# A second-level product for pairs of values units, rope pairs in another order, and a table of priority shifts

## The chip, the cores and the metric

The kernel runs on one core of a Trainium2 chip. The metric is the time of one execution in microseconds, as the device reports it; below 0.2% two versions of this kernel can't be told apart. Five engines work beside each other, each through its own instructions in order: PE (TensorE, matmuls), DVE (VectorE), ACT (ScalarE), POOL (GpSimd) and SP (SyncE, which issues the transfers here).

## The reference, cut to what matters

Two requests of 512 tokens go through the same trunk of two layers, a differential attention and a two-way retention. Each begins with one wide projection of the normalised input, and this projection is what the change is about:

```python
def trunk(x, ...):
    h = rms_norm(x, norm_g[0], NORM_EPS)
    x = x + diff_attention(h, da_w_in[0], ..., da_w_out[0], lambda_init)
    h = rms_norm(x, norm_g[1], NORM_EPS)
    x = x + bidir_retention(h, ret_w_in[0], ..., ret_w_out[0])
    return rms_norm(x, final_norm_g, NORM_EPS)

# in either mixer
proj = h @ w_in                      # 512 x 1024 by 1024 x 8192 (layer 1) or 6144 (layer 2)
q, k, v, gate = jnp.split(proj, ...) # q, k are rotated; v is used as it is; silu(gate) scales the output
```

All is float32. The two requests share the weights, so the projection is one product with 1024 tokens.

## The kernel before

**Products.** A float32 value is split into an upper part and a rest (`hi_of` on ACT, `lo_of` on DVE), and a product is three matmul passes (`PASSES`: upper by upper, upper by rest, rest by upper). On top of that the projection uses Strassen's scheme in Winograd's form: tokens, the 1024 rows of the weights and a unit's columns are halved, and a unit needs seven products P1 to P7 of half size instead of eight (`SEQ`). The token side is prepared once per layer by `make_b`, in blocks B11, B21, T1, T2, B22, T3, T4 (`B_OF`). The weights' side (sums and differences of quarters, then the split) is prepared by `Unit.prep` for each product.

**Units.** A unit is a strip of weight columns with one purpose. *Rope* units hold q or k, which are rotated (`rot_done`); *gate* units hold the gate (`gate_done`); both are of kind "pair", and their products are 12 matmuls of 128x512. *Wide* units hold values (`v_done`): they take the tokens as the stationary side, are twice as broad, and a product is 48 matmuls of 128x256 in two banks.

**Second level.** Two rope units next to each other share P2 (the product with B21): a `Duo` sees their two strips of weights as one matrix, applies Winograd's scheme once more, and does two P2 (24 matmuls of 128x512) as seven inner products of 6 matmuls of 128x256. Its operands are prepared in parts D0 to D3 (`Duo.part`) from the strips' quarters a11 to a22; the token side is cut by `inner_blocks` into t1 to t4. Wide units and single gates do P2 in full.

**Order of the units.** `mixed` puts five gates first, then the ropes in twos, with a wide unit or a gate between, and two gates last. With R, g and w for a rope, gate and wide unit the layers read

```
layer 1: g g g g g  RR w  RR g  RR RR w  RR w  RR RR w  RR  g g
layer 2: g g g g g  RR w g  RR w  RR w  RR w  g g
```

`product_order` lays out the products: a unit's last one, P4, stands behind the first of the next unit ("tail"). `projections` prepares weights ahead of PE as long as the tiles of the prepared products fit into `PROJ_WS` buffers (ws); the raw weights land in four buffers of 512 KB before that (`raw_t`).

**What sets the order on the engines.** Nothing runs at once: each operation goes to a `Plan` with its cost and what it reads and writes. `Plan.arrange` then lays the operations out by a list scheduler: PE keeps its order but for a window, the other engines take the ready operation that is due first, where the due time is counted back from the PE products that need it. `Plan.issue` repeats this eight times, keeps the shortest layout and writes the instructions out in that order, engine by engine. The order on each engine is fixed then.

**Banks.** Results stand in eight banks: three "pj", two "sc", two "o", one "tp". P1, P6, P7 and P4 of a unit add up in a pj bank (two for a wide unit), P5 and P3 in sc, P2 in o. A bank is free again when ACT and DVE have read it. P4 is handed over in its bank: `v_done` reads it twice, by `hi_of` (L439) and `lo_of` (L442).

**Lines of the profile.** L712 is a product of a rope or gate unit, L722 one of a wide unit, L874 an inner product of a Duo, L1318 the transposes of x for `make_b`, L502 its blocks. L773 adds a product to a kept one. L442 is `lo_of`, L439 `hi_of`, L425 and L423 are scalings on DVE and ACT, L1194 is the power that turns a row's sum of squares into its scale, on POOL. L1155 is the output projection, L1160 adds its result to x.

## Time and profile before

| what | value |
|---|---|
| median of 3 runs | 1796.06 us (1795.7 to 1797.08) |
| the profiled execution | 1796.09 us, its span 1794.1 us |
| busy: PE, PEld, DVE, ACT, POOL | 99%, 88%, 85%, 51%, 7% |
| instructions: PE, DVE, ACT, POOL | 10533, 2635, 1952, 256 |
| HBM | 209.55 MB read, 117.44 MB written |

The stages are, by PE's timeline: start and first projection to 640 us, attention with its output projection to 1021, second projection to some 1470, retention and the end. How to read: a row of a timeline gives start, length and engine, the line of the kernel, what is written from what, the tile's shape and the count, and in brackets how long the engine was idle before and who ended that. Matmuls are pipelined, so their price is the distance between starts.

### The profile page before, as it was taken

The page shows a single profiled execution, that of the slowest core. Times are in us where ns is not written, and L with a number is a line of the kernel's source. Part 1 is how long each engine was busy: PE and PEld are TensorE (multiplying, and loading weights), DVE is VectorE, ACT ScalarE, POOL GpSimd, SP SyncE. Part 2 cuts the span into 40 slices and gives each one's busy share as a digit, 9 for nine tenths or more (in the row PEclk, how much of TensorE's full clock was granted, in tenths as well). Part 3 has the DMA queues.
Part 4 walks back from the last instruction along what each step waited for, and adds up shares of the span by engine and source line. Part 5 has one row for each costly group of instructions (what it writes and reads, how often), then busy time and mean ns, then how long its engine had stood idle before and what let it go on. Part 6 is the DMA issues. An engine that isn't in the chain of part 4 may idle for free.

```text
span 1794.1 us, 28748 instructions
## 1 busy us (share of the span) xinstructions
PE 1778.4 (99%) x10533; PEld 1569.9 (88%) x10533; DVE 1532.6 (85%) x2635; ACT 917.8 (51%) x1952; POOL 120.6 (7%) x256
## 2 busy tenths in 40 slices
PE   9999999999999999999999999999999999999998
PEld 7789888989899888888888878898989988888887
DVE  8978899887897888888888798887988977888887
ACT  8664454444444555555455776444444455444446
POOL 1000000000000011111111200000000000111114
PEclk9999999999999999999999999999999999999999
DMA  6336454546364695555453524473746569664652
GB/s 219 120 114 196 153 170 141 181 149 202 112 181 164 196 350 184 186 188 188 168 187 127 188 65 159 130 236 105 235 139 225 165 216 404 238 234 176 229 217 94
DMA packets 162821, 328.86 MB, mean 183 GB/s; under 512 B 12773, under 2 KB 76921, under 8 KB 162681
## 3 DMA queue, kind: packets, MB, share of 16 engines
q1 hardware_dynamic: 162352, 326.71, 53.7%
q8 instruction: 82, 1.34, 0.3%
q14 instruction: 59, 0.48, 0.1%
q10 hardware_dynamic: 328, 0.34, 0.1%
HBM read 209.55 MB, written 117.44 MB: 182 GB/s over the span
## 4 chain that ended last, share of the span: by engine, by line
PE 89%; DVE 6%; DMA 2%; issue 1%; ACT 1%; SPq 1%; POOL 0%; DVEq 0%; POOLq 0%; ACTq 0%
PE pj L712 20%; PE pj L1155 19%; PE sc L712 11%; PE pj L722 6%; PE o L712 5%; PE o L1483 5%; PE sc L1422 5%; PE o L874 3%; PE sc L722 3%; PE o L1692 2%; PE o L722 2%; DVE ws L442 1%; PE sc L1648 1%; PE tp L1672 1%; PE o L1700 1%
## 5 line engine op out<-in xcount | busy, mean ns | idle before, releaser
L1155 PE MATMUL pj<-ws,arena 128*128 128x512 f32 x1542 | 377.9, 392 | 0.0
L1155 PEld LDWEIGHTS pj<-ws,arena 128*128 128x128 f32 x1542 | 281.8, 188 | 54.6 <-DVE m L989 0.3
L712 PE MATMUL pj<-b,ws 128*128 128x512 f32 x1080 | 263.1, 391 | 0.0
L712 PEld LDWEIGHTS pj<-b,ws 128*128 128x128 f32 x1080 | 199.5, 188 | 39.8
L439 ACT CAST ws<-st 128x512 fp32r<-128x512 f32 (+1 forms) x260 | 153.4, 601 | 145.9 <-PE o L874 42.1
L1160 DVE SCALAR_TENSOR_TENSOR b<-pj,pad,b 128x512 f32<-128x512 f32 (+1 forms) x257 | 191.1, 746 | 26.0 <-PE pj L1155 23.6
L442 DVE TENSOR_TENSOR ws<-st,ws 128x512 fp32r<-128x512 f32 (+1 forms) x260 | 169.0, 662 | 28.1 <-ACT ws L439 26.4
L712 PE MATMUL sc<-arena,ws 128*128 128x512 f32 x768 | 185.8, 390 | 0.0
L442 DVE TENSOR_TENSOR ws<-raw,ws 128x512 fp32r<-128x512 f32 (+2 forms) x177 | 139.8, 798 | 34.8 <-ACT ws L439 30.5
L712 PEld LDWEIGHTS sc<-arena,ws 128*128 128x128 f32 x768 | 143.1, 188 | 29.5
L712 PE MATMUL pj<-arena,ws 128*128 128x512 f32 x636 | 156.8, 391 | 1.9 <-DVE os L442 1.9
L712 PEld LDWEIGHTS pj<-arena,ws 128*128 128x128 f32 x636 | 118.1, 188 | 27.5 <-DVE os L442 2.7
L439 ACT CAST ws<-raw 128x512 fp32r<-128x512 f32 (+2 forms) x177 | 125.5, 715 | 30.7 <-PE pj L712 5.8
L1440 ACT ACTIVATE b<-sc,pad 128x512 f32<-128x512 f32 x128 | 87.4, 691 | 72.2 <-DVE pad L1430 72.0
L765 ACT COPY c<-pj 128x512 f32<-128x512 f32 x104 | 61.0, 587 | 121.7 <-PE pj L712 89.9
L722 PE MATMUL pj<-ws,b 128*128 128x256 f32 x960 | 116.9, 275 | 0.0
L722 PEld LDWEIGHTS pj<-ws,b 128*128 128x128 f32 x960 | 113.3, 188 | 0.6
L712 PE MATMUL o<-arena,ws 128*128 128x512 f32 x456 | 108.6, 390 | 3.0 <-DVE b L502 1.8
L712 PEld LDWEIGHTS o<-arena,ws 128*128 128x128 f32 x456 | 85.1, 188 | 21.1 <-ACT ws L439 2.0
L439 ACT CAST os<-e 128x512 fp32r<-128x512 f32 x96 | 59.2, 622 | 83.0 <-DVE e L773 33.9
L1422 PE MATMUL sc<-arena 128*128 128x512 f32 x384 | 101.6, 398 | 0.0
L1483 PEld LDWEIGHTS o<-arena 128*128 128x128 f32 x768 | 93.0, 188 | 2.5
(255 smaller groups left out, 3060.7 us busy)
## 6 DMA issues: line engine op xcount, KB each, us to landing
qk<-os SPq DMA_DIRECT2D x192, 256.0 KB, 3.6
arena<-qk SPq DMA_DIRECT2D x96, 512.0 KB, 6.8
v<-os SPq DMA_DIRECT2D x64, 512.0 KB, 4.3
arena<-v SPq DMA_DIRECT2D x64, 512.0 KB, 4.1
raw<-in_da_w_in_dram SPq DMA_DIRECT2D x63, 512.0 KB, 4.1
raw<-in_ret_w_in_dram SPq DMA_DIRECT2D x48, 512.0 KB, 4.3
os<-g SPq DMA_DIRECT2D x32, 512.0 KB, 7.6
g<-e SPq DMA_DIRECT2D x48, 256.0 KB, 3.7
```

The costliest lines, as they stand in the source:

```text
L439: act(n, lambda: nc.scalar.copy(dst(), src()), r, w)
L442: dve(n, lambda: nc.vector.tensor_tensor(dst(), src(), hi().bitcast(F32), op=ALU.subtract), r, w)
L712: nc.tensor.matmul(ps.t, a[u][0]()[:, k, :], bt[k][:, v, :], start=(opens and k == 0 and i == 0), stop=(k == 3 and i == 2), skip_group_che ...
L722: nc.tensor.matmul(ps[:, (t % 2) * 256:(t % 2) * 256 + 256], bt[k][:, v, t * P:(t + 1) * P], a[u][0]()[:, k, :], start=(opens and t % 2 == ...
L765: act(S, lambda c=c, ps=ps: nc.scalar.copy(c.t, ps.t), [ps], [c])
L874: nc.tensor.matmul(ps[:, c0:c0 + 256], w[:, lo:lo + P], of(b, j), start=(start and j == 0 and i == 0), stop=(j == 1 and i == 2), skip_grou ...
L1155: nc.tensor.matmul(ps[:, here], o[a][:, e, t * P:(t + 1) * P], u[b][:, e, here], start=(m == 0), stop=(m == 5))
L1160: axpy(n, lambda half=half, here=here, ps=ps: nc.vector.scalar_tensor_tensor(half, ps[:, here], rr[:, t % 2:t % 2 + 1], half, op0=ALU.mult ...
L1422: nc.tensor.matmul(s.t, q[:, a, t * P:(t + 1) * P], k[:, b, :], start=(n == 0), stop=(n == 2))
L1440: act(840, lambda j=j, s=s, m=m: nc.scalar.activation(p[:, j, :], s.t, AF.Exp, bias=m.t, accum_out=sm[:, 2 * j + n:2 * j + n + 1]), [s, m] ...
L1483: nc.tensor.matmul(o[:, e * 256:(e + 1) * 256], v[b][:, j, e * P:(e + 1) * P], aT[a][:, j, :], start=(n == 0), stop=(n % 12 == 11), skip_g ...
L1692: nc.tensor.matmul(o[:, e * 256:(e + 1) * 256], v_[v][:, 2 * c + j, e * P:(e + 1) * P], a_[:, u, j * 256:(j + 1) * 256], start=(e == 0 and ...
```

## The change

A class `WideDuo` does for two wide units what `Duo` does for ropes: their two P2 (96 matmuls) become seven inner products of 12 matmuls of 128x256 each, grouped as E1 to E4. Each inner product is added at once (DVE) to the four kept tiles of P1, so those of the first unit now stay in an `e` buffer (`keeps`). Four differences and sums of weight quarters (128x512) are added and seven half-size splits take the place of two full ones per unit.

For this the wide units stand in twos (`mixed`), which makes the order of the units

```
layer 1: g g g g g  RR ww  RR  RR g  RR  RR  RR ww  RR  RR  g g
layer 2: g g g g g  RR ww  RR g  RR ww  RR  g g
```

The rope pairs take their products in another order: P5, P6, P3 and P7 of the first unit now come ahead of P1 of the second, and the Duo's D1 and D3 later. Duo's operands are split in larger pieces (D0 whole, D2 whole). `PROJ_WS` goes from six to five, and the place of the sixth tile is shared by a fifth landing buffer for raw weights (`both_ring`). Behind the eight layouts, `Plan.issue` now goes through a table of 36 entries: each draws random shifts (a fixed seed) for the due times of a share of the operations off PE around one time of the plan, and lays all out again; the shifts add up.

```diff
--- before.py
+++ after.py
 WS_BUFS = 7
-PROJ_WS = 6
+PROJ_WS = 5
...
+SHIFTS = (
+    (636.05, 8, 4, 0.5, 513480), (1015.01, 4, 1, 1, 179848), (1470.58, 30, 0.3, 0.5, 986431),
...
+)
...
-        self.best = best
+        out, span, begin, starts = best
+        shift = {}
+        for at, back, by, part, seed in SHIFTS:
+            rng = random.Random(seed)
+            for n, e in out:
+                if e != "PE" and at - back <= begin[n] <= at + 6.0 and rng.random() < part:
+                    shift[n] = shift.get(n, 0.0) + rng.gauss(0.0, by)
+            out, begin, span = self.arrange(starts, shift)
...
-        rings.append(ar.tile([P, 1024 + 32 if last else RING], F32R, tag=f"ws{i}", name=f"ws_{i}"))
+        rings.append(None if i == PROJ_WS else ar.tile([P, 1024 if last else RING], F32R, tag=f"ws{i}", name=f"ws_{i}"))
+        if i == PROJ_WS:
+            ar.tile([P, RING], F32R, tag="both", name="both")
...
+    def both_ring(dt):
+        cnt[0] += 1
+        label = f"both_{cnt[0]}"
+        return ar.tile([P, RING], dt, tag="both", name=label)
+
     def ws_t(shape, lo=0, bufs=PROJ_WS):
...
-            t = rings[i][:, lo:lo + 1024]
+            t = (both_ring(F32R) if i == PROJ_WS else rings[i])[:, lo:lo + 1024]
...
-    def raw_t(shape):
-        return work("raw", shape, 4)
+    def raw_t(shape, bufs=4):
+        n = math.prod(shape[1:])
+        def make(i):
+            t = view(wk, "raw", i, n, [P, n]) if i < 4 else both_ring(F32)[:, 0:n]
+            return t.rearrange("p (a b) -> p a b", a=shape[1])
+        b = Buf(plan, f"raw{bufs}", bufs, make)
+        i = b.nth % bufs
+        b.also = Buf(plan, "ring5" if i == 4 else f"rawplace{i}", 1, None)
+        return b
...
-            self.n_ws = 2 if self.wide else 1
...
+        def needs(self, op):
+            return 2 if self.wide else 1
...
-                    c = c_t()
+                    c = e_t() if self.keeps and op == "P1" else c_t()
...
-            w = self.w[op] = ws_t([P, 1024], 4 if op in ("D1", "D3") else 36)
-            if op == "D0":
-                for k, src in enumerate((a11, a12)):
-                    hi, lo = (lambda k=k, u=u: four(w[:, u * 512 + k * 256:u * 512 + k * 256 + 256]) for u in range(2))
-                    hi_of(256, hi, src, [xu], [(w, (0, k))])
-                    lo_of(256, lo, src, hi, [xu, (w, (0, k))], [(w, (1, k))])
-                return
-            if op == "D3":
-                hi, lo = (lambda u=u: four(w[:, u * 512 + 256:u * 512 + 512]) for u in range(2))
-                hi_of(256, hi, a22, [xv], [(w, (0, 1))])
-                lo_of(256, lo, a22, hi, [xv, (w, (0, 1))], [(w, (1, 1))])
-                hi, lo = (lambda u=u: w[:, u * 512:u * 512 + 256] for u in range(2))
-                s3 = lambda: self.late[:, 256:512]
-                hi_of(256, hi, s3, [(self.late, 1)], [(w, (0, 0))])
-                lo_of(256, lo, s3, hi, [(self.late, 1), (w, (0, 0))], [(w, (1, 0))])
+            w = self.w[op] = ws_t([P, 1024], 36)
+            if op in ("D0", "D3"):
+                src, key, n = (self.raw(u, 0, 4), xu, S) if op == "D0" else (a22, xv, 256)
+                hi, lo = (lambda u=u: w[:, u * 512:u * 512 + n].rearrange("p (k j i) -> p k j i", k=n // P, j=2)
+                          for u in range(2))
+                hi_of(n, hi, src, [key], [(w, 0)])
+                lo_of(n, lo, src, hi, [key, (w, 0)], [(w, 1)])
                 return
             x = st_t([P, S])
             if op == "D1":
                 s1 = put(x, 0, a21, a22, ALU.add, [xv])
                 self.s2 = put(x, 1, s1, a11, ALU.subtract, [xu, (x, 0)]), (x, 1)
             else:
-                self.late = x
-                put(x, 0, a12, self.s2[0], ALU.subtract, [xu, self.s2[1]])
-                put(x, 1, a11, a21, ALU.subtract, [xu, xv])
-                hi, lo = (lambda u=u: w[:, u * 512:u * 512 + 256] for u in range(2))
-                s4 = lambda: x[:, 0:256]
-                hi_of(256, hi, s4, [(x, 0)], [(w, (0, 0))])
-                lo_of(256, lo, s4, hi, [(x, 0), (w, (0, 0))], [(w, (1, 0))])
-                return
+                put(x, 0, a11, a21, ALU.subtract, [xu, xv])
+                put(x, 1, a12, self.s2[0], ALU.subtract, [xu, self.s2[1]])
             hi, lo = (lambda u=u: w[:, u * 512:u * 512 + 512] for u in range(2))
-            hi_of(S, hi, lambda: x.t, [x], [(w, (0, None))])
-            lo_of(S, lo, lambda: x.t, hi, [x, (w, (0, None))], [(w, (1, None))])
+            hi_of(S, hi, lambda: x.t, [x], [(w, 0)])
+            lo_of(S, lo, lambda: x.t, hi, [x, (w, 0)], [(w, 1)])
...
+    class WideDuo:
+        PARTS = dict(E1=("a12", "a11"), E2=("s1", "s2"), E3=("s3", "s4"), E4=("a22",))
+        def __init__(self, u, v):
+            self.u, self.v, self.w = u, v, {}
+            u.keeps = True
+        def needs(self, op):
+            return len(self.PARTS[op])
+        def prep(self, op):
+            u, v = self.u, self.v
+            if op == "E1":
+                self.a = {}
+                for name, x in (("a1", u), ("a2", v)):
+                    t, key = x.take(0, 1)
+                    for k in range(2):
+                        self.a[f"{name}{k + 1}"] = (lambda t=t, k=k: t()[:, 2 * k:2 * k + 2]), key
+            for name in self.PARTS[op]:
+                if name[0] == "s":
+                    a, b = dict(s1=("a21", "a22"), s2=("s1", "a11"), s3=("a11", "a21"), s4=("a12", "s2"))[name]
+                    x, a, b = st_t([P, 2, 256]), self.a[a], self.a[b]
+                    fn = ALU.add if name == "s1" else ALU.subtract
+                    dve(S, lambda x=x, a=a, b=b, fn=fn: nc.vector.tensor_tensor(x.t, a[0](), b[0](), op=fn),
+                        [a[1], b[1]], [x])
+                    self.a[name] = (lambda x=x: x.t), x
+                src, key = self.a[name]
+                w = self.w[name] = ws_t([P, 2, 2, 256], 28)
+                hi_of(S, lambda w=w: w[:, 0], src, [key], [(w, 0)])
+                lo_of(S, lambda w=w: w[:, 1], src, lambda w=w: w[:, 0], [key, (w, 0)], [(w, 1)])
+        def inner(self, name, block, ps, start=False):
+            w = self.w[name]
+            plain = block[0] == "b"
+            bt = [Bop["B21", k] for k in range(4)] if plain else [Bop["B21", block]]
+            def of(v, j, t):
+                if plain:
+                    c = 256 * (block == "b22") + t * P
+                    return bt[2 * (block in ("b21", "b22")) + j][:, v, c:c + P]
+                return bt[0][:, v, j, t * P:(t + 1) * P]
+            def fn():
+                for t in range(2):
+                    for j in range(2):
+                        for i, (a, b) in enumerate(PASSES):
+                            nc.tensor.matmul(ps[:, t * 256:t * 256 + 256], of(b, j, t), w[:, a, j],
+                                             start=(start and t == 0 and j == 0 and i == 0), stop=(j == 1 and i == 2),
+                                             skip_group_check=True)
+            pe(1.367, fn, [w, *bt], [ps])
+        def product(self, op):
+            u, v = self.u, self.v
+            cu, cv = u.s["c1"], v.s["c1"]
+            def add(e, ps):
+                dve(S, lambda: nc.vector.tensor_tensor(e.t, ps.t, e.t, op=ALU.add), [ps, e], [e])
+            if op == "E1":
+                first, self.near = bank("o"), bank("o")
+                self.inner("a12", "b21", first, True)
+                add(cu[0], first)
+                self.inner("a11", "b11", self.near, True)
+                add(cu[0], self.near)
+            elif op == "E2":
+                self.far = bank("o")
+                self.inner("s1", "t1", self.far, True)
+                add(cv[1], self.far)
+                self.inner("s2", "t2", self.near)
+                add(cu[1], self.near)
+            elif op == "E3":
+                self.inner("s3", "t3", self.near)
+                add(cv[1], self.near)
+                self.inner("s4", "b22", self.far)
+                add(cu[1], self.far)
+                u.done(0, 0, cu, u.s, False)
+            else:
+                self.inner("a22", "t4", self.near)
+                add(cv[0], self.near)
+                v.done(0, 0, cv, v.s, False)
...
+            if v and u.kind == v.kind == "wide":
+                left.pop(0)
+                d = WideDuo(u, v)
+                out += [(u, "P1"), tail, (u, "P5"), (u, "P6"), (u, "P3"), (u, "P7"), (u, "P4"), (v, "P1"), (d, "E1"),
+                        (d, "E2"), (d, "E3"), (v, "P5"), (d, "E4"), (v, "P6"), (v, "P3"), (v, "P7")]
+                tail = (v, "P4")
+                continue
             if v and u.kind == v.kind == "pair" and u.done.__qualname__ == v.done.__qualname__:
                 left.pop(0)
                 d = Duo(u, v)
-                out += [(u, "P1"), tail, (v, "P1"), (u, "P5"), (d, "D1"), (u, "P6"), (u, "P3"), (d, "D3"), (u, "P7"), (v, "P5"), (u, "P4"), (v, "P6"), (v, "P3"), (v, "P7")]
+                out += [(u, "P1"), tail, (u, "P5"), (u, "P6"), (u, "P3"), (u, "P7"), (v, "P1"), (d, "D1"), (v, "P5"),
+                        (d, "D3"), (u, "P4"), (v, "P6"), (v, "P3"), (v, "P7")]
...
-                if sum(w.n_ws for w, _ in order[n:ready]) + v.n_ws > PROJ_WS:
+                if sum(w.needs(q) for w, q in order[n:ready]) + v.needs(p) > PROJ_WS:
...
-        others = [u for both in itertools.zip_longest(wides, gates) for u in both if u]
+        others = [wides[:2], gates, wides[2:]]
         groups, m = len(ropes) // n, len(others)
         for k in range(groups):
             share = -(-(k + 1) * m // groups) + (-k * m // groups)
-            out += ropes[k * n:(k + 1) * n] + [others.pop(0) for _ in range(share)]
+            out += ropes[k * n:(k + 1) * n] + [u for _ in range(share) for u in others.pop(0)]
```

In the whole program PE has 10476 rows' worth of matmuls and branches instead of 10524: 48 of 128x256 fewer. DVE has 80 operations of 128x512 more, 48 of 128x256, 8 of 128x1024 fewer and one scaling of 128x1024 more.

**Where a wide unit ends and a rope pair begins** (PE, first projection). `pj`, `sc` and `o` are banks, `ws` weight tiles, `b` and `arena` the token side. Before, the third such place:

```order
L722 MATMUL pj_365<-ws_80,b_842 128x256
L722 MATMUL pj_365<-ws_78,b_857 128x256 x2
L722 MATMUL pj_365<-ws_80,b_857 128x256
L712 MATMUL pj_294<-arena,ws_82 128x512 x12
L712 MATMUL sc_330<-arena,ws_84 128x512 x12
L874 MATMUL o_306<-arena,ws_86 128x256 x6
```

And now, the first of two in this layer:

```order
L763 MATMUL pj_294<-ws_80,b_856 128x256
L763 MATMUL pj_294<-ws_78,b_859 128x256 x2
L763 MATMUL pj_294<-ws_80,b_859 128x256
L753 MATMUL sc_252<-arena,ws_82 128x512 x12
L753 MATMUL pj_362<-b_653,ws_84 128x512 x3
L753 MATMUL pj_362<-b_661,ws_84 128x512 x3
L753 MATMUL pj_362<-arena,ws_84 128x512 x6
```

Before, the product behind the wide unit's P4 writes pj_294, one of the two pj banks that the wide unit has just filled (the other is pj_365). Now it writes an sc bank, and the pj bank behind it is the one that the first rope unit holds already.

**The first inner products of two wide units** (DVE, first projection; there was no such place). The rows with L998 add a bank to a kept tile, L683 are sums of weight quarters, L481 is `lo_of`:

```order
L998 TENSOR_TENSOR e_703<-o_334,e_703 128x512
L683 TENSOR_TENSOR st_500<-raw_266,raw_270 128x512
L481 TENSOR_TENSOR ws_76<-st_494,ws_76 128x512
L998 TENSOR_TENSOR e_703<-o_306,e_703 128x512
L481 TENSOR_TENSOR ws_84<-st_491,ws_84 128x512
L998 TENSOR_TENSOR c_543<-o_334,c_543 128x512
L481 TENSOR_TENSOR ws_80<-st_496,ws_78 128x512
L481 TENSOR_TENSOR ws_80<-st_500,ws_78 128x512
L998 TENSOR_TENSOR e_246<-o_306,e_246 128x512
```

Each add frees one of the two o banks, in turns, and other work for the products that follow stands between the adds.

**The start of the second projection** (the engine that scales the last tile of x, b_233). Before it was ACT:

```order
L423 ACTIVATE b_231<-b_231,pad_77 128x1024
L1186 ACTIVATE c_594,pad_77<-b_233 128x512
L1187 ACTIVATE pad_77<-pad_77,pad_79 128x1
L439 CAST arena<-m_449 128x512
L1187 ACTIVATE pad_77<-pad_77 128x1
L439 CAST arena<-m_470 128x512
L439 CAST arena<-m_254 128x512
L423 ACTIVATE b_9357<-b_233,pad_77 128x1024
L439 CAST arena<-m_441 128x512
```

Now it is DVE:

```order
L481 TENSOR_TENSOR ws_82<-b_9131,ws_82 128x512
L464 TENSOR_SCALAR b_231<-b_231,pad_77 128x1024
L464 TENSOR_SCALAR m_448<-sc_252,pad_79 128x512
L481 TENSOR_TENSOR ws_84<-raw_270,ws_84 128x512
L464 TENSOR_SCALAR b_9346<-b_233,pad_77 128x1024
L481 TENSOR_TENSOR arena<-m_473,arena 128x512
L481 TENSOR_TENSOR arena<-m_448,arena 128x512
```

The scalings of b_231 and b_233 have left ACT; b_232 went the other way. On PE the transposes that read these tiles now stand behind two products of the projection instead of three.

30 lines of the change are left out of this document (17 added, 13 removed), and 10 rows, old and new, of the table SHIFTS.

## The prediction

> **What bounds the kernel now.** The page comes first: spans, the shares of the engines, the granted clock and the chain that ended last.
>
> ```profile
> span 1794.1 us, 28748 instructions
> PE 1778.4 (99%) x10533; PEld 1569.9 (88%) x10533; DVE 1532.6 (85%) x2635; ACT 917.8 (51%) x1952; POOL 120.6 (7%) x256
> ...
> PEclk9999999999999999999999999999999999999999
> ...
> PE 89%; DVE 6%; DMA 2%; issue 1%; ACT 1%; SPq 1%; POOL 0%; DVEq 0%; POOLq 0%; ACTq 0%
> ```
>
> PE (TensorE) is busy for 1778.4 of 1794.1 us at a full clock, and it holds 89% of the chain. So the time is the matmuls plus what PE loses, 15.7 us of idle. DVE has 85% on average, so a stage in which it has more to do than PE can still make PE wait. Where the idle is, the view by windows of 25 us shows (columns: window, length, then busy time of PE, PEld, DVE, ACT, POOL, then clock and DMA).
>
> ```profile
> 25.00:50.00 25.00, 23.16 (x118) 18.86 (x117) 24.21 (x44) 19.62 (x36) 2.35 (x3) 1.00 0.15 49
> ...
> 275.00:300.00 25.00, 25.00 (x123) 21.20 (x122) 25.00 (x47) 12.48 (x24) 0.00 (x0) 1.00 0.44 129
> 300.00:325.00 25.00, 25.00 (x131) 21.41 (x131) 24.67 (x42) 9.73 (x16) 0.00 (x0) 1.00 0.61 179
> ...
> 1025.00:1050.00 25.00, 22.55 (x115) 18.64 (x115) 22.80 (x38) 19.49 (x38) 3.42 (x1) 1.00 0.11 42
> ...
> 1775.00:1800.00 25.00, 12.46 (x61) 10.39 (x59) 12.64 (x22) 14.33 (x41) 10.63 (x12) 0.87 0.38 147
> ```
>
> The last window is the tail behind the last matmul, which the change does not touch. The others are the start of each layer's projections. From 275 to 325 two rope pairs follow each other; DVE is busy for 49.67 of 50 us there, and PE still loses nothing. The list of PE's waits names who ended the most of the idle time (columns: total us, times, longest).
>
> ```profile
> PE pj L712 <- DVE os L442: 1.9, 3, 0.8
> PE o L712 <- DVE b L502: 1.8, 1, 1.8
> ```
>
> **The matmuls.** In the program's order PE has 48 matmuls with a 128x256 result fewer: per pair of wide units two P2 of 48 each become seven inner products of 12 each, 96 to 84, and there are four pairs. All other shapes keep their counts. The price is the distance from start to start in PE's timeline, since a single matmul's own duration overlaps the next.
>
> ```profile
> 176.18 5.60 PE L722 MATMUL sc<-ws,arena 128*128 128x256 f32 x48
> 181.62 5.60 PE L722 MATMUL pj<-ws,b 128*128 128x256 f32 x48
> 187.06 2.91 PE L712 MATMUL pj<-arena,ws 128*128 128x512 f32 x12
> 189.81 5.64 PE L722 MATMUL pj<-ws,b 128*128 128x256 f32 x48
> 195.49 3.04 PE L712 MATMUL pj<-arena,ws 128*128 128x512 f32 x12
> ...
> 360.66 5.64 PE L722 MATMUL pj<-ws,b 128*128 128x256 f32 x48
> 366.99 3.02 PE L712 MATMUL pj<-arena,ws 128*128 128x512 f32 x12 [0.69 <-DVE os L442]
> ...
> 372.57 1.59 PE L874 MATMUL o<-arena,ws 128*128 128x256 f32 x12
> 373.99 0.87 PE L874 MATMUL o<-b,ws 128*128 128x256 f32 x6
> ...
> 437.63 5.64 PE L722 MATMUL pj<-ws,b 128*128 128x256 f32 x48
> 444.10 3.04 PE L712 MATMUL pj<-arena,ws 128*128 128x512 f32 x12 [0.83 <-DVE os L442]
> ...
> 552.50 5.64 PE L722 MATMUL pj<-ws,b 128*128 128x256 f32 x48
> 558.48 3.02 PE L712 MATMUL pj<-arena,ws 128*128 128x512 f32 x12 [0.34 <-DVE os L442]
> ```
>
> From 176.18 to 181.62 are 5.44 us for 48, or 0.1133 each. So 48 fewer are **-5.4 us**. The trace has no wide inner products yet. The pair's inner products (L874) take 1.42 us for 12, 0.118 each; if the 336 new ones cost that, the gain shrinks by 336 x 0.005 = 1.7 us to -3.8. I take -5.4, since the new ones stand behind other 128x256 matmuls with a block of B as weights, as in the L722 rows.
>
> **The exit of a wide unit.** In the same rows a wide unit's last product should take 5.44 us; to the next start it takes 5.68, 6.33, 6.47 and 5.98 us (from 189.81, 360.66, 437.63, 552.50). That is 0.24 + 0.89 + 1.03 + 0.54 = 2.7 us lost, at the four places in layer 1 where rope units follow a wide one. What is late is named: DVE's second half of the split (L442) that empties the wide unit's pj bank, which the next product, P1 of the second rope unit, wants at once. In the new order P5 of the first rope unit stands there, in an sc bank, and P1 of the second comes four products later, some 11 us by 2.75 us each (187.06 to 189.81). The exits into ropes also fall from four to two. The sc banks were emptied behind P3 of the wide unit, three products earlier, so nothing else is late: **-2.7 us**, bounds -2.7 and 0.
>
> **The start of layer 1.**
>
> ```profile
> 39.25 3.01 PE L712 MATMUL sc<-arena,ws 128*128 128x512 f32 x12
> 42.88 0.65 PE L1318 MATMUL tp<-ident,b 128*128 128x128 f32 x4 [0.62 <-DVE arena L502]
> ...
> 43.73 3.01 PE L712 MATMUL o<-arena,ws 128*128 128x512 f32 x12
> 47.96 2.34 PE L712 MATMUL o<-arena,ws 128*128 128x512 f32 x9 [1.22 <-DVE arena L502]
> ```
>
> Twelve 128x512 matmuls take some 2.75 us; to the next start stand 3.63 and 4.23 us, so about 0.9 and 1.5 are lost to DVE, which empties banks of transposes too late. Of the operations that stand between the first emptying of this run and the one that ends the second loss, the new DVE order has two of 128x512 fewer: the lower half of a weight tile and that of a block of B now stand behind it. That is 2 x 0.60 (priced below) = **-1.2 us**. Bounds: 0 and -2.4.
>
> **The start of layer 2.** PE's, ACT's and POOL's rows:
>
> ```profile
> 1029.81 0.49 PE L1318 MATMUL sc<-ident,b 128*128 128x128 f32 x3
> 1030.97 0.33 PE L1318 MATMUL sc<-ident,b 128*128 128x128 f32 x1 [0.67 <-ACT b L423]
> ...
> 1032.01 0.60 PE L1318 MATMUL o<-ident,b 128*128 128x128 f32 x4
> 1032.44 0.60 PE L1318 MATMUL tp<-ident,b 128*128 128x128 f32 x4
> 1034.82 5.50 PE L712 MATMUL o<-arena,ws 128*128 128x512 f32 x23 [1.78 <-DVE b L502]
> ```
>
> ```profile
> 1014.45 0.54 POOL L1194 TENSOR_TENSOR pad<-pad 128x1 f32<-128x1 f32 x1 [1.47 <-ACT pad L1187]
> ...
> 1026.31 3.42 POOL L1194 TENSOR_TENSOR pad<-pad 128x1 f32<-128x1 f32 x1 [4.05 <-ACT pad L1187]
> ```
>
> ```profile
> 1029.77 1.15 ACT L423 ACTIVATE b<-b,pad 128x1024 f32<-128x1024 f32 x1 [2.56 <-POOL pad L1194]
> ```
>
> A group of four transposes takes 0.43 us (1032.01 to 1032.44), so 0.8 us are lost at 1030.97 and 1.9 at 1034.82. The cause is one step back: POOL's power of one row statistic took 3.42 us where the one before took 0.54, ACT waited 2.56 us to scale the last x tile, and everything behind it on ACT was late, then DVE. In the new order DVE scales this tile and one before it: ACT has 1.15 us less ahead of the statistic, and nothing on ACT waits behind it. On DVE the scaling waits for POOL, and the lower halves of the first blocks of B wait behind it. The tile was ready at 1029.77 + 1.15 = 1030.92; with a power of 0.54 and without the 1.15 it is ready at 1030.92 - 2.88 - 1.15 = 1026.9. But PE transposes after two products instead of three, so it wants the tile 2.75 us before 1029.81 + 0.33 = 1030.14, at 1027.4. It comes in time, with 0.5 us to spare; I leave 0.4 of loss for DVE's own queue: 2.7 - 0.4 = **-2.3 us**. Bounds: -2.7, and 0 (the power again at 3.42 loses 2.4 here, and the second loss stays in part).
>
> The Trainium skill, "SBUF — State Buffer", section "Who interferes with whom", says that a DVE instruction with two inputs in SBUF shuts out a GpSimd instruction that reads SBUF for its whole length. The trace agrees: the 3.42 us ended as a run of such subtractions did. By that rule a DVE that waits for POOL frees it after one instruction, 0.60 us, and the loss stays near 0.4; were the length POOL's own, the other bound would be the likelier one and the sum 1789.0.
>
> **What the change adds.** DVE's operations, start to start:
>
> ```profile
> 360.02 0.68 DVE L773 TENSOR_TENSOR e<-pj,c 128x512 f32<-128x512 f32 x1
> 360.62 0.68 DVE L442 TENSOR_TENSOR ws<-st,ws 128x512 fp32r<-128x512 f32 x1
> 361.22 0.42 DVE L442 TENSOR_TENSOR ws<-raw,ws 128x256 fp32r<-128x256 f32 x1
> 361.56 0.42 DVE L822 TENSOR_TENSOR st<-raw 128x256 f32<-128x256 f32 x1
> ```
>
> A 128x512 operation holds DVE for 0.60 us, a 128x256 one for 0.34. The order has 80 more of the first, 48 fewer of the second and 7 fewer of 128x1024, whose price is at most two of 128x512: +48 - 16.3 - 8.4 = +23 us of DVE, nearly all in the wide pairs, some 6 each. A wide pair lasts 12 x 5.44 + 7 x 1.36 = 74.8 us and DVE's work in it is about 49 us, so it fits as a sum. Inside the first five inner products it is tight: each adds into SBUF before its bank can be used again two products (1.36 us between) later, and eight DVE operations (4.8 us) must fall into the 5.4 us from the first product's end. With one foreign operation ahead of each add, an add comes 0.2 us late once per pair: **+0.8 us** for four, bounds 0 and 2.4 (one 0.60 late each).
>
> The longer runs of rope pairs are the other cost. By the code a rope pair gives DVE 60 operations of 128x512 and 10 of 128x256, 39.4 us, and PE 12 x 2.75 + 7 x 0.71 = 38.0: DVE falls back by about 1.4 us a pair, and gates and wide units let it catch up. Before, two pairs in a row were the most in layer 1, and the windows at 275 and 300 show that they cost PE nothing. Now three stand in a row, and the weights are prepared five tiles ahead instead of six, which takes one product, 2.75 us, off the cushion. Bounds: 0, and 3 runs x 2.75 + 1.4 = 9.7. Nearest are the windows without a loss; I take the third pair's own **+1.4 us**. The fifth landing buffer, the reordered pairs and the table of shifts add no work: SP issues 773 transfers before and after, and PE's other matmuls keep their counts. ACT gets 52 copies of 128x512 more, 48 of 128x256 and 8 of 128x1024 fewer; at 51% it hides them.
>
> **Sum.** -5.4 - 2.7 - 1.2 - 2.3 + 0.8 + 1.4 = -9.4 us. The profiled execution took 1796.09 us, 2.0 beside its span, and the median of the runs is 1796.06; so 1796.1 - 9.4 = **1786.7 us**.
>
> **Rivals.** (a) The losses go almost wholly: the table of shifts takes the rest at both starts and hides the adds. -5.4 - 2.7 - 2.3 - 2.7 = -13.1, 1783.0 us. For it speaks that each loss is one late operation that a different order can bring forward; against it, the 1.2 us that PE waits at the very start for x, whose rows are the same. (b) The losses only move: PE does less, and DVE, busier by 23 us, makes it wait as long elsewhere. 1796.1 - 5.4 = 1790.7, or 1792.3 with the dearer inner products. For it speaks DVE at 49.67 of 50. (c) Slower: the cushion ahead of rope pairs is gone. The place is layer 1; the price is for each of its eight pairs the deficit of 1.4 us and the 2.75 us that the sixth tile covered, 8 x 4.15 = 33.2, less the 1.4 counted. It decides once 9.4 + 3.6 = 13 us of it come, four tenths; at half, the time is 1786.7 + 15.9 = 1802.6. Against it stand the windows at 275 to 325. (d) The change does not do what it says: the count of matmuls is in the order, so only the price is open, and (b) has it.
>
> **Chances.** The forecast 0.55, (a) 0.2, (b) 0.18, (c) 0.07. The range takes in (a) and most of (b): 1782.5 to 1793. A measurement of this kernel tells about 0.2%, 3.6 us, from no change, so faster means below 1792.5: 0.86; within 0.2%: 0.08; slower 0.06.
>
> **What would show it.** PE's matmul count 48 lower and the new inner products 0.113 us apart; no wait of pj on os (L442) at a wide exit; at the second start under 1 us lost; PE at 25.00 in nearly all windows with three rope pairs. Wrong would be: idle PE with DVE at 25.00 in those windows, or the E products apart by over 1.6 us. The first means that (c) begins, the second that the adds are late.

## The result, and the profile after

The changed kernel takes 1785.75 us (median of 4 runs, 1785.57 to 1786.69); the kernel before, run beside it, 1796.13 us (1795.7 to 1797.08). The ratio is 0.9939, 95% interval [0.9925, 0.9954]: 10.4 us faster, where 9.4 were predicted. Spans compare as 1783.5 and 1794.1 us. The page of the changed kernel, its spans, shares and the chain that ended last:

```profile
span 1783.5 us, 28682 instructions
...
PE 1771.9 (99%) x10485; PEld 1564.4 (88%) x10485; DVE 1555.7 (87%) x2659; ACT 923.7 (52%) x1948; POOL 115.7 (6%) x256
...
PE 94%; DVE 3%; DMA 2%; issue 0%; ACT 0%; SPq 0%; ACTq 0%; POOL 0%; POOLq 0%; DVEq 0%
```

PE has 48 matmuls fewer, its share of the chain went from 89 to 94%, and DVE's from 6 to 3% although DVE is busy 23 us longer. If one sums every place at which two starts on PE stand over 0.15 us further apart than usual for that line and shape, the kernel before lost 10.4 us and this one 4.7. The list of PE's waits after the change (total us, times, longest) shows what is left:

```profile
PE sc L1407 <- DVE pad L491: 1.2, 1, 1.2
PE sc L1769 <- DMA arena<-qk: 0.9, 1, 0.9
PE tp L1466 <- ACT b L462: 0.7, 1, 0.7
PE sc L1466 <- DVE b L464: 0.5, 1, 0.5
```

The waits of pj on os and of o on b are gone. Three of these four stand in the first 12 us. The second is new: the retention's first score product (sc) waits for a load. Three of the windows that were shown of before, one inside the three rope pairs that now follow each other, and the start of the retention (columns as there):

```profile
25.00:50.00 25.00, 24.97 (x126) 20.63 (x125) 24.79 (x47) 20.54 (x40) 3.29 (x4) 1.00 0.23 74
275.00:300.00 25.00, 25.00 (x132) 21.51 (x131) 24.93 (x47) 10.59 (x19) 0.00 (x0) 1.00 0.53 151
350.00:375.00 25.00, 25.00 (x112) 20.68 (x111) 25.00 (x44) 11.40 (x20) 0.00 (x0) 1.00 0.60 169
1025.00:1050.00 25.00, 25.00 (x119) 20.69 (x118) 25.00 (x42) 17.50 (x31) 0.00 (x0) 1.00 0.11 43
1475.00:1500.00 25.00, 24.31 (x167) 22.51 (x168) 19.47 (x35) 14.18 (x34) 2.45 (x4) 1.00 1.03 410
```

At 25 and at 1025 PE was busy for 23.16 and 22.55 us before; now it loses next to nothing in either. The three rope pairs in a row stand from some 320 to 433 us, and in all four windows from 325 to 425 PE is at 25.00 while DVE is at 24.83 to 25.00. At 1475 the DMA engines are busy all the time (share 1.03), and PE waits for them. PE's rows of one block of the new inner products (L988) and of the exit of that pair of wide units into ropes:

```profile
190.84 2.88 PE L988 MATMUL o<-ws,arena 128*128 128x256 f32 x24
193.56 1.52 PE L988 MATMUL o<-ws,b 128*128 128x256 f32 x12
195.04 1.64 PE L988 MATMUL o<-ws,ws 128*128 128x256 f32 x12
196.53 1.52 PE L988 MATMUL o<-ws,arena 128*128 128x256 f32 x12
197.88 1.29 PE L763 MATMUL sc<-ws,arena 128*128 128x256 f32 x10
...
225.11 5.64 PE L763 MATMUL pj<-ws,b 128*128 128x256 f32 x48
230.59 0.62 PE L753 MATMUL sc<-arena,ws 128*128 128x512 f32 x2
```

The first two inner products take 2.72 us for 24 matmuls, 0.1133 each: the lower price of the two that were possible. The next two stand 1.48 and 1.49 us apart instead of 1.36: each waits some 0.12 us for the add two products earlier (the second add ends on DVE at 194.89 us, and the product that needs its bank starts at 195.04). The wide unit's last product takes 5.48 us to the next start (225.11 to 230.59), so nothing is lost at the exit.

Term by term, measured as the distance of PE's starts at the same places:

| term | predicted | measured |
|---|---|---|
| 48 matmuls | -5.4 | -5.4 |
| wide exits, layer 1 | -2.7 | -2.6, nothing left |
| start of layer 1 | -1.2 | -2.0 (2.2 lost before, 0.2 now) |
| start of layer 2 | -2.3 | -2.8, nothing left |
| adds in the four blocks | +0.8 | +0.9 |
| longer rope runs, five tiles | +1.4 | 0 in the rope pairs |
| start of the retention | not foreseen | +1.0 |
| first gates (70 us, 0.4) and start of the attention (0.7) | not foreseen | +1.1 |

These add up to -9.8. PE's last matmul starts 11.2 us earlier (1776.00 against 1787.18), so another 1.4 us lie in distances too small to count singly. Behind that matmul the program takes 0.6 us longer (7.51 us against 6.95; it is 6.9 to 8.2 in the runs below), which leaves the 10.6 us between the spans.

### The profile page after: what moved, and what is told of

The parts are those of the page before. It is cut to its first block, busy times and chain, and to the rows that moved or that the text cites. A ratio compares the mean times of both kernels' runs of the same rounds, so it can differ in the third digit from the quotient of the medians.

```text
span 1783.5 us, 28682 instructions
## 1 busy us (share of the span) xinstructions
PE 1771.9 (99%) x10485; PEld 1564.4 (88%) x10485; DVE 1555.7 (87%) x2659; ACT 923.7 (52%) x1948; POOL 115.7 (6%) x256
## 4 chain that ended last, share of the span: by engine, by line
PE 94%; DVE 3%; DMA 2%; issue 0%; ACT 0%; SPq 0%; ACTq 0%; POOL 0%; POOLq 0%; DVEq 0%
PE pj L753 21%; PE pj L1276 20%; PE sc L753 11%; PE pj L763 10%; PE sc L763 5%; PE o L1604 5%; PE sc L1543 5%; PE o L753 4%; PE o L902 3%; PE o L1813 3%; PE o L988 2%; PE sc L1769 1%; PE tp L1793 1%; PE o L1821 1%; PE pj L1584 1%; PE tp L1584 1%
## 5 line engine op out<-in xcount | busy, mean ns | idle before, releaser
L1276 PE MATMUL pj<-ws,arena 128*128 128x512 f32 (+1 forms) x1334 | 352.2, 392 | 0.0
L1276 PEld LDWEIGHTS pj<-ws,arena 128*128 128x128 f32 x1334 | 244.9, 188 | 47.6
L478 ACT CAST ws<-st 128x512 fp32r<-128x512 f32 x264 | 161.1, 621 | 169.7 <-PE sc L753 32.8
L481 DVE TENSOR_TENSOR ws<-st,ws 128x512 fp32r<-128x512 f32 x264 | 178.2, 686 | 51.2 <-ACT ws L478 35.1
L478 ACT CAST ws<-raw 128x512 fp32r<-128x512 f32 (+2 forms) x140 | 103.3, 740 | 62.7 <-PE o L902 22.6
L481 DVE TENSOR_TENSOR ws<-raw,ws 128x512 fp32r<-128x512 f32 (+2 forms) x135 | 109.2, 813 | 25.5 <-ACT ws L478 21.4
L806 ACT COPY c<-pj 128x512 f32<-128x512 f32 x96 | 56.5, 588 | 81.7 <-PE pj L753 56.9
L1604 PE MATMUL o<-arena 128*128 128x256 f32 x768 | 93.6, 277 | 0.0
```

What stands on the lines that cost most here:

```text
L478: act(n, lambda: nc.scalar.copy(dst(), src()), r, w)
L481: dve(n, lambda: nc.vector.tensor_tensor(dst(), src(), hi().bitcast(F32), op=ALU.subtract), r, w)
L806: act(S, lambda c=c, ps=ps: nc.scalar.copy(c.t, ps.t), [ps], [c])
L1276: nc.tensor.matmul(ps[:, here], o[a][:, e, t * P:(t + 1) * P], u[b][:, e, here], start=(m == 0), stop=(m == 5))
L1604: nc.tensor.matmul(o[:, e * 256:(e + 1) * 256], v[b][:, j, e * P:(e + 1) * P], aT[a][:, j, :], start=(n == 0), stop=(n % 12 == 11), skip_g ...
```

## The experiments

Most start from the changed kernel without its table (e1), some from the kernel before. Every ratio is to the kernel before, whose median was 1796.1 to 1796.5 in these comparisons.

| run | edit | median us | ratio, 95% interval |
|---|---|---|---|
| e1 | no table | 1786.44 | 0.9944 [0.9932, 0.9957] |
| e2 | no table, no inner products | 1794.19 | 0.9989 [0.9980, 0.9998] |
| e3 | no table, P1 of the second rope early | 1786.50 | 0.9945 [0.9931, 0.9958] |
| e4 | before, new rope order | 1793.32 | 0.9984 [0.9976, 0.9993] |
| e5 | before, DVE scales the last rows | 1794.86 | 0.9993 [0.9985, 1.0002] |
| e6 | no table, six rope pairs in a row | 1788.22 | 0.9954 [0.9939, 0.9969] |
| e7 | no table, limit of three tiles | 1786.74 | 0.9947 [0.9933, 0.9960] |
| e8 | no table, four landing buffers | 1787.89 | 0.9949 [0.9935, 0.9963] |
| e9 | table without its late entries | 1784.49 | 0.9935 [0.9921, 0.9949] |
| e10 | no table, adds twice | 1795.97 | 0.9997 [0.9987, 1.0006] |
| e11 | before, five weight tiles | 1792.81 | 0.9981 [0.9972, 0.9990] |
| e12 | before, five tiles and new rope order | 1791.51 | 0.9973 [0.9963, 0.9984] |

The intervals reach some 2 us either way, and single runs of one kernel differ by 1 to 2 us. So a difference of 1 us between two of these kernels is read at its place in the trace, not from the medians.

### What the table and the inner products are worth

```diff
-SHIFTS = ( ... )
+SHIFTS = ()
```

> The changed kernel with an empty table of shifts; all else as after. Theory (the inner products, the order of the units and the rope order bring 5.4 of matmuls and 2.7 at the wide exits by themselves; what the starts and the adds cost depends on the order on DVE, ACT and POOL, so the table is what brought the rest): 1796.1 - 5.4 - 2.7 = 1788.0 us, and up to 1791 if the adds between the inner products come late without the table; no wait of PE pj on DVE os at a wide exit. The loss at the start of layer 2 should be back at 1 to 3 us. Rival (the table is worth nothing, the gain is all in the structure): 1785.7 to 1786.5, PE's idle time as after, some 4.5 us.

The theory fell, the rival holds: 1786.44 us, 0.7 more than with the table. At the start of layer 2, 0.65 us are lost without the table, not 1 to 3, and at the start of layer 1 0.32. The gain is nearly all in the structure. Two more things show beside the sum. Each of the 28 inner products takes 1.36 us in e1 (and in e3, e6 and e7), so without the table the adds cost nothing; they come late in the order that the table leaves on DVE. And PE loses 0.5 us at 289 us, in the second rope pair behind the wide units, where it waits for a Duo's weights (L469). PE's and DVE's busy time in that window of e1, 24.63 and 25.00 us:

```profile
275.00:300.00 25.00, 24.63 (x129) 21.07 (x128) 25.00 (x47) 11.13 (x20) 0.00 (x0) 1.00 0.62 168
```

```diff
-d = WideDuo(u, v)
-out += [(u, "P1"), tail, (u, "P5"), ..., (d, "E1"), (d, "E2"), (d, "E3"), (v, "P5"), (d, "E4"), ...]
+out += [(u, "P1"), tail, (u, "P2"), (u, "P5"), ..., (u, "P4"), (v, "P1"), (v, "P2"), (v, "P5"), ...]
```

> As the run without the table, and the two wide units of a pair do their P2 in full (48 matmuls of 128x256 more in all, no kept tiles in e, no adds per inner product); the order of the units and of the rope products stays. To be read against the run without the table. Theory (48 matmuls at 0.1133 us, adds hidden): 5.4 us slower than without the table. Rival 1 (the adds cost as predicted 0.2 us per block): 4.6 us slower. Rival 2 (the inner products without the table wait for their adds, over 0.6 us a block): less than 3 us slower, and the run without the table shows PE o on DVE among its waits.

It is 7.8 us slower than e1, more than any of the three said. 5.4 are the matmuls. The other 2.4 are places that the plan lays out differently when this work is gone: PE loses 1.2 us more at 473 us, inside the second pair of wide units, and the start of layer 2 has its old losses back. PE's waits and POOL's last power in e2:

```profile
PE o L741 <- DVE b L529: 1.8, 1, 1.8
...
PE pj L751 <- DVE e L802: 1.1, 1, 1.1
```

```profile
1024.40 3.40 POOL L1302 TENSOR_TENSOR pad<-pad 128x1 f32<-128x1 f32 x1 [5.25 <-ACT pad L1295]
```

### The power on POOL at the start of layer 2

In the kernel before, the scaling of the last two row tiles is given to DVE:

```diff
+if g == 1 and t >= 2:
+    plan.op("DVE", 0.07 + 0.00058 * D, lambda: nc.vector.tensor_scalar(q.t, x.t, r.t, None, op0=ALU.mult), [x, r], [q])
+else:
     evac(D, lambda: q.t, lambda: x.t, lambda: r.t, [x, r], [q], 0.00058)
```

> The kernel before, with one edit: the last two x tiles at the start of layer 2 are scaled by DVE only, not by whichever of ACT and DVE the plan picks. Theory (DVE's runs of subtractions with two inputs in SBUF hold POOL's power; a DVE that waits for the power lets it through): the last power takes under 1 us instead of 3.42, the two losses of 0.8 and 1.9 us at the start of layer 2 shrink to under 1 us in all, 1796.1 - 2.0 = 1794.1 us. Rival (the power is slow by itself, or the loss comes from DVE's own queue): the power stays over 3 us or the 1.9 us stay, 1795.5 to 1797.

In the kernel before, DVE subtracted without a stop from 1025.63 to 1029.32 us, and POOL's power (1026.31 to 1029.73) ended behind it:

```profile
1026.23 1.89 DVE L442 TENSOR_TENSOR arena<-m,arena 128x512 fp32r<-128x512 f32 x3
1028.03 1.29 DVE L648 TENSOR_TENSOR st<-st,raw 128x512 f32<-128x512 f32 x2
```

DVE's rows in e5, and POOL's power in the same microseconds:

```profile
1027.39 0.68 DVE L648 TENSOR_TENSOR st<-raw,raw 128x512 f32<-128x512 f32 x1
1027.99 1.29 DVE L442 TENSOR_TENSOR arena<-m,arena 128x512 fp32r<-128x512 f32 x2
1029.71 0.75 DVE L1512 TENSOR_SCALAR b<-b,pad 128x1024 f32<-128x1024 f32 x1 [0.44 <-POOL pad L1194]
```

```profile
1028.08 1.60 POOL L1194 TENSOR_TENSOR pad<-pad 128x1 f32<-128x1 f32 x1 [5.26 <-ACT pad L1187]
```

POOL starts while DVE subtracts, and it ends 0.40 us after DVE's last subtraction (1029.68 against 1029.28); that one comes sooner, since DVE now stops to wait for the power. The power takes 1.60 us instead of 3.42, and the two losses of 2.8 us become one of 1.2. That is the theory's mechanism; its "under 1 us" for the power was too low, as three subtractions were still ahead of the stop. The Trainium skill's rule that such instructions of DVE shut out GpSimd ("SBUF — State Buffer", section "Who interferes with whom") agrees with this row. The median is 1.6 us lower, but the interval takes in no change, and the profiled execution lost 2.3 us more at the wide exits; so the place shows the effect, and the time alone does not.

In the changed kernel the last power starts while DVE scales:

```profile
1018.04 0.74 DVE L464 TENSOR_SCALAR m<-sc,pad 128x512 f32<-128x512 f32 x1
1018.70 0.68 DVE L481 TENSOR_TENSOR ws<-raw,ws 128x512 fp32r<-128x512 f32 x1
1019.30 0.75 DVE L464 TENSOR_SCALAR b<-b,pad 128x1024 f32<-128x1024 f32 x1
```

```profile
1018.35 0.54 POOL L1315 TENSOR_TENSOR pad<-pad 128x1 f32<-128x1 f32 x1 [4.21 <-ACT pad L1308]
```

### Two cures for the wide exits, one for the start of layer 1

In the kernel before, the products of a rope pair in the new order:

```diff
-out += [(u, "P1"), tail, (v, "P1"), (u, "P5"), (d, "D1"), (u, "P6"), ...]
+out += [(u, "P1"), tail, (u, "P5"), (u, "P6"), (u, "P3"), (u, "P7"), (v, "P1"), (d, "D1"), ...]
```

> The kernel before, with one edit: the products of a rope pair stand in the new order. Theory (the exits' 2.7 us go, nothing else is late): 1796.1 - 2.7 = 1793.4 us, the wait of PE pj on DVE os gone at 366, 443 and 558 us; the starts of both layers lose what they lost before (2.2 to 2.7 us each). Rival (the loss only moves to another bank or to the Duo's inner products): 1795.5 to 1796.5, with a new wait of 0.5 us or more near those places.

1793.32 us, and PE has no wait of pj on os left: the theory's place and size. The reverse, in the changed kernel without its table:

```diff
-out += [(u, "P1"), tail, (u, "P5"), (u, "P6"), (u, "P3"), (u, "P7"), (v, "P1"), (d, "D1"), ...]
+out += [(u, "P1"), tail, (v, "P1"), (u, "P5"), (u, "P6"), (u, "P3"), (u, "P7"), (d, "D1"), ...]
```

> As the run without the table, but P1 of a pair's second rope unit stands behind the tail again, as before, the other products in the new order. To be read against the run without the table by PE's waits. Theory (the exit's loss was P1 of the second rope wanting the pj bank that lo_of empties): a wait of PE pj on DVE os comes back at the two exits of wide pairs in layer 1, 0.3 to 1.0 us each, 0.6 to 2.0 us in all, nothing else changes by over 1 us. Rival (the exits are free because the pair of wide units ends with less work on DVE): no such wait, time as without the table within 0.5 us.

Here the theory falls. PE's rows at the first exit of e3, the wide unit's last product and P1 of the second rope right behind it:

```profile
225.79 5.64 PE L751 MATMUL pj<-ws,b 128*128 128x256 f32 x48
231.26 2.91 PE L741 MATMUL pj<-arena,ws 128*128 128x512 f32 x12
```

5.47 us, no loss, and 1786.50 us. So something else in the change cures the exits as well. In the kernel before, sums and splits of weights for later products stand ahead of the late split on DVE. The number of tiles should limit how many of them can, so the kernel before gets one tile fewer:

```diff
-PROJ_WS = 6
+PROJ_WS = 5
```

> The kernel before with five weight tiles instead of six, nothing else. Theory (at the start of layer 1 the sixth tile's preparation on DVE stands ahead of the emptying of transposes, so fewer tiles cure that start): the losses at 42 and 46 us fall from 2.2 us to under 0.6, 1796.1 - 1.7 = 1794.4 us if the shorter lead costs nothing elsewhere. Rival (the start is cured by the other parts of the change): these losses stay over 1.5 us, 1796 to 1798 us.

The theory holds at the start of layer 1, and the time falls by more than it said, to 1792.81 us: the exits at 366, 443 and 558 us lose nothing either, though 0.8 and 0.5 are lost at two others (194 and 1375 us, where the kernel before loses 0.2 and nothing) and 0.5 at 70. The split for which PE waits at the exit at 366 us, before and then in e11:

```profile
366.25 0.69 DVE L442 TENSOR_TENSOR os<-pj,os 128x512 fp32r<-128x512 f32 x1
```

```profile
363.65 0.69 DVE L442 TENSOR_TENSOR os<-pj,os 128x512 fp32r<-128x512 f32 x1 [0.46 <-ACT os L439]
```

It starts 2.6 us earlier, while PE is only 0.6 us ahead there (360.03 against 360.66 at the start of the wide unit's last product). DVE's rows at the start of layer 1, of the kernel before and then of e11:

```profile
42.77 0.75 DVE L502 SCALAR_TENSOR_TENSOR arena<-o,pad,arena 128x512 fp32r<-128x512 f32 x1
43.43 0.68 DVE L442 TENSOR_TENSOR ws<-st,ws 128x512 fp32r<-128x512 f32 x1
...
45.35 0.68 DVE L442 TENSOR_TENSOR ws<-st,ws 128x512 fp32r<-128x512 f32 x1
45.95 1.29 DVE L442 TENSOR_TENSOR b<-b,b 128x512 fp32r<-128x512 f32 x2
47.16 0.74 DVE L502 SCALAR_TENSOR_TENSOR arena<-o,pad,arena 128x512 fp32r<-128x512 f32 x1
```

```profile
42.09 0.75 DVE L502 SCALAR_TENSOR_TENSOR arena<-o,pad,arena 128x512 fp32r<-128x512 f32 x1
42.76 0.68 DVE L648 TENSOR_TENSOR st<-st,raw 128x512 f32<-128x512 f32 x1
...
44.67 0.68 DVE L442 TENSOR_TENSOR b<-b,b 128x512 fp32r<-128x512 f32 x1
45.27 0.74 DVE L502 SCALAR_TENSOR_TENSOR arena<-o,pad,arena 128x512 fp32r<-128x512 f32 x1
```

In the kernel before two halves of weight tiles (ws) and two of blocks of B (b) stand between the emptyings of transposes (L502; two more of these are left out in either cut). With five tiles it is one weight sum (L648) and one half of a block, and the last emptying, for which PE waits, comes 1.9 us earlier. The edit is the number of tiles alone, so that is the cause; that no tile was free yet for the two halves is argued, not shown. Both edits together, in the kernel before:

> The kernel before with five weight tiles and the new order of the rope products, nothing else. Each alone took 2.8 to 3.5 us. Theory (both cure the same loss at the wide exits, and only five tiles cure the start of layer 1): exits 2.5 to 2.7 and start 1.9 less, 0.5 lost anew at 70 us as in the run with five tiles, 1792.0 us, no wait of PE pj on DVE os left. Rival (each frees DVE somewhere of its own, so they add up): 1789.5 to 1790.5.

1791.51 us: 4.9 less than before, where the two alone took 2.8 and 3.4 (6.2 if they added up). No wait of pj on os is left. It is nearer to the theory than to the rival: the cures share the exits, though not to the last half us.

### The lead of the weights, and the runs of rope pairs

```diff
+limit = 3 if units is first_units and 56 < n < 134 else PROJ_WS
-if sum(w.needs(q) for w, q in order[n:ready]) + v.needs(p) > PROJ_WS:
+if ready > n and sum(w.needs(q) for w, q in order[n:ready]) + v.needs(p) > limit:
```

> As the run without the table, but from layer 1's rope pairs on weights are prepared three tiles ahead instead of five (layer 1 only). Theory (a tile less is 2.75 us less lead; in the changed kernel the weights are ready 3 to 9 us before PE wants them in rope pairs and 0.4 us at the tightest place, so two tiles less are felt at about half of the pairs): 3 to 12 us slower than without the table, PE waiting for DVE ws. Rival (the lead is set by DVE's order, not by the number of tiles): within 1 us of the run without the table.

1786.74 us, but this decides nothing: the edit moved no instruction on any engine. The loop's limit sets only in which order operations are handed to the plan; what lets a tile be filled early is the number of buffers, and that was still five. The run is a second measurement of e1, 0.3 us from the first.

```diff
 others = [wides[:2], gates, wides[2:]]
+if len(ropes) > 10:
+    return out + ropes[:2] + wides[:2] + ropes[2:4] + wides[2:] + gates + ropes[4:] + end
```

> As the run without the table, but the units of layer 1 stand ggggg RR ww RR ww g and then six rope pairs in a row, where the changed kernel has at most three. Theory (DVE has some 1.7 us more to do in a rope pair than PE, and falls back on the outputs first: weights stay 6 to 9 us ahead, rotations are put off until their buffers run out): a loss from the fourth pair on, three times 1.7 = 5 us, 1791.5 us, PE waiting for DVE e or c there. Rival (the deficit is none, DVE is busy 25.00 of 25 only because it has no wait): 1786.0 to 1787.0, PE at 25.00 in all windows of the six pairs.

1788.22 us, between the two. Two of the windows of the six pairs, and PE's rows in the sixth:

```profile
450.00:475.00 25.00, 25.00 (x131) 21.50 (x130) 25.00 (x46) 11.04 (x21) 0.00 (x0) 1.00 0.54 148
...
550.00:575.00 25.00, 23.80 (x121) 19.98 (x120) 25.00 (x47) 10.65 (x20) 0.00 (x0) 1.00 0.61 167
```

```profile
571.34 0.50 PE L890 MATMUL o<-b,ws 128*128 128x256 f32 x2 [0.44 <-DVE st L677]
572.60 0.75 PE L890 MATMUL o<-b,ws 128*128 128x256 f32 x4 [0.76 <-DVE ws L469]
```

DVE is full, yet five pairs go through without a loss; the first comes in the sixth, 1.5 us (0.60 and 0.92 by the starts). Where the deficit goes meanwhile shows when each product is matched with the operations that feed it and that it feeds. For each of the six pairs, in us: how long before a product its weights are complete on DVE (median, and the least of the pair), and how long after its product a rotation is completed (median):

```
pair         1     2     3     4     5     6
weights    8.6   8.0   8.4   8.1   6.4   5.3
least      4.6   3.4   4.1   2.4   0.1   0.1
rotations  9.7  13.5  16.3  19.0  20.8  24.5
```

The weights keep most of their lead for four pairs; the rotations, which nothing waits for, fall back by some 3 us a pair. That is the theory's mechanism with a longer reach than it gave. The three pairs in a row of the changed kernel stay inside it: their rotations come 13.3, 16.8 and 16.9 us after their products, and the least lead is 3.7 us. The changed kernel's tightest place is the second pair behind the first two wide units, at 282 us, where the rotations come 25.8 us after their products and the least lead is 1.0 us; there e1 loses its 0.5. From 225 to 585 us the median lead of its pairs is 6.7 to 8.8 us, in the kernel before 9.1 to 11.1.

```diff
-r = ... raw_t([P, 4, 256], 5)
+r = ... raw_t([P, 4, 256], 4)
```

> As the run without the table, but raw weights land in four buffers as before, not five. Theory (the loads land early enough, so the fifth buffer brings nothing in these runs): within 0.7 us of the run without the table. Rival (with five tiles of lead the loads need the fifth buffer): over 2 us slower, with a wait of ACT or DVE for the raw loads ahead of a late weight tile.

1787.89 us, 1.4 more than e1 and so between the two; the rival's wait is there at one place. PE's row:

```profile
479.61 1.64 PE L976 MATMUL o<-ws,b 128*128 128x256 f32 x12 [1.45 <-ACT ws L466]
```

DVE waited 2.05 us for raw weights just before. By the starts PE loses 1.6 us there. The fifth landing buffer covers that wait for the inner products' weights, in one block of four.

### How much room the adds have

```diff
 dve(S, lambda: nc.vector.tensor_tensor(e.t, ps.t, e.t, op=ALU.add), [ps, e], [e])
+dve(S, lambda: nc.vector.scalar_tensor_tensor(e.t, ps.t, 0.0, e.t, op0=ALU.mult, op1=ALU.add), [ps, e], [e])
```

> As the run without the table, but each inner product of a wide pair is added by two DVE operations, the second adding zero times the bank, 0.66 us more each (28 of them, 18.5 us of DVE). In the changed kernel an add ends 0.15 to 0.47 us before the next but one inner product wants its bank, at three places of a block. Theory (the adds have no more room than that): 0.2 to 0.5 us lost at each of these places, 3 to 5.5 us slower than without the table, PE o waiting for DVE e or c. Rival (the plan finds other room): within 1 us.

1795.97 us: 9.5 slower than e1, well over what the theory gave. PE's rows in the first block:

```profile
191.22 2.88 PE L976 MATMUL o<-ws,arena 128*128 128x256 f32 x24
194.82 1.64 PE L976 MATMUL o<-ws,b 128*128 128x256 f32 x12 [0.71 <-ACT ws L466]
197.22 1.64 PE L976 MATMUL o<-ws,ws 128*128 128x256 f32 x12 [0.76 <-DVE e L987]
```

From the second to the fifth, the inner products take 2.24, 2.40, 1.80 and 1.48 us to the next start instead of 1.36, which is 2.5 us a block: not the adds alone are late, but behind them on DVE the next inner product's weights too. One operation more per inner product takes back the whole gain.

### The new wait at the retention, and a faster version

```diff
-    ... (1470.58, 30, 0.3, 0.5, 986431), ... (1469.41, 30, 2, 1, 333010), ... (1466.42, 4, 2, 1, 641057), ...
-    ... (1471.8, 30, 4, 1, 444217), ... (1465.85, 16, 1, 1, 247190), ... (1482.91, 30, 2, 0.2, 965717), ...
```

> The changed kernel with its table less the six entries around 1466 to 1483 us; up to there the order on every engine is that of the changed kernel. Theory (the wait of 1.04 us for the first k at the start of the retention comes from how these entries order PE's products and the queue of transfers there): the wait is under 0.3 us, 1785.75 - 1.0 = 1784.7 us. Rival (it comes from the order of the units: the last rope pair's outputs are stored right ahead of these loads): the wait stays at 0.5 to 1.2 us, 1785.5 to 1786.3.

1784.49 us (1784.27 to 1785.46; none of its runs reaches the changed kernel's 1785.57, though the two were not run beside each other). PE's rows in the changed kernel and then in e9:

```profile
1473.94 0.86 PE L1793 MATMUL tp<-arena 128*128 128x256 f32 x6
1475.69 0.98 PE L1769 MATMUL sc<-arena 128*128 128x256 f32 x6 [0.88 <-DMA arena<-qk]
```

```profile
1471.38 0.86 PE L1791 MATMUL tp<-arena 128*128 128x256 f32 x6
1472.08 2.89 PE L751 MATMUL pj<-b,ws 128*128 128x512 f32 x12
1475.02 0.93 PE L1767 MATMUL sc<-arena 128*128 128x256 f32 x6
```

With the six entries the score (sc) stands ahead of a product of 2.75 us and waits for its k; without them the product comes first and covers the load. 0.2 us are still lost, so the place shows 0.8 of the 1.3 us between the medians.

## Why the prediction was right, point by point

The time was right within 1 us, and part of that is luck. The six terms of the sum came to -11.9 us where -9.4 was said, chiefly because the longer rope runs cost nothing and the start of layer 1 gave more. Losses of 2.1 us that no term named and the longer end (0.6), less the 1.4 us of small distances, make it the -10.6 of the spans.

- **The matmuls.** Right in price and count. e2 adds that taking the inner products out costs 7.8 us, because the plan then lays out other places differently; the 5.4 are the share of the matmuls.
- **The wide exits.** The size was right, the reason only half. The step said that P1 of the second rope wants the bank at once, and that the new order removes this. e4 shows that the order alone is enough. But e3 puts P1 back and loses nothing, and e11 cures three exits without touching the order. The split was late because DVE did sums and splits of later weights ahead of it. A later P1 cures all exits (e4); one tile fewer cures three in the kernel before and loses more at two others (e11).
- **The start of layer 1.** The mechanism was right, the size 0.8 us too small. The step counted two DVE operations fewer ahead of the last emptying. Between the emptying at 42.77 us and the last one stood two halves of weight tiles and two of blocks of B, and in the changed kernel (42.32 to 44.90) one half of a block: three fewer, 1.8 us. e11 ties it to the sixth tile.
- **The start of layer 2.** Right: the power is held by DVE's subtractions (e5). The 0.4 us that the step left for DVE's own queue did not come. What e1 and e2 show beside this is that it hangs on which operation DVE happens to have there: the power takes 0.91 us in e1, 3.40 in e2.
- **The adds.** +0.8 predicted, +0.9 measured, at the places that were named, but that is luck in part: the step took the lateness for a cost of the structure, and without the table there is none (e1). Two adds a block come 0.12 us late in the changed kernel because of the order that the table leaves on DVE. e10 shows how little room is left.
- **The longer rope runs.** This is the step that failed: "DVE falls back by about 1.4 us a pair" and one product "off the cushion", +1.4 in all. DVE does fall back, but on rotations, which have over 20 us of room (e6), and the three pairs in a row lose nothing. The missing tile does cost something, elsewhere: some 0.5 us at 70 us, in every run with five tiles and in none with six (the kernel before, e4, e5). And it was booked as a cost alone; in e11 it makes the kernel before 3.4 us faster, since DVE no longer prepares weights ahead of work for which PE waits. The sign that the prediction named for being wrong, idle PE beside a full DVE, appears without the table: the 0.5 us at 289 us in e1. Rival (c), which priced each of eight pairs at 4.15 us, falls with e6: six in a row lose 1.5 us, all in the sixth.
- **The table** was counted as no work, and one rival gave it the rest of both starts. It is worth 0.7 us in all by the medians. It removes losses at 289 us, at the start of layer 2 and at the start of the attention; it adds 0.9 at the adds, and its late entries add 1.0 by a wait for a DMA that the prediction did not look for. It adds no transfers: both traces have 771 (the step has 773 for both).

What stays open: how the 0.7 us at the start of the attention come about, by what step one tile fewer costs 0.5 us at 70 us, and why e12 is half a us below the theory.

## What to carry to other kernels

A deeper lead of prepared operands is no free cover where the engine that prepares them also frees banks: look for what stands ahead of the late operation, and try one buffer fewer before a new order. A busy engine at 25.00 of 25 says nothing of who pays: find which of its outputs has a waiter, and measure how far the others may fall behind. An experiment on a limit has to change the resource that binds; compare the order of the instructions before reading a time from it.

## What the runs showed of the hardware

One 128x1 power on POOL took 0.54, 0.91, 1.60, 3.40 and 3.42 us in these runs; in the three longest it ended some 0.4 us after a run of DVE's subtractions did, however long that run was. At the start of the retention the DMA engines are busy all the time, at 410 GB/s by the window above, and there a load that the changed kernel issued at 1469.02 us, 5.6 us before PE wanted its k (at 1474.65, one 0.71 us product after 1473.94), came 1.0 us late.
